# Eight attention heads as one four-phase pipeline, and TensorE's order written down, in a hybrid decoder layer

## The chip, the cores and the metric

The kernel runs on one core of a Trainium2 chip. The metric is the device time of one execution in microseconds (us). The engines are named as in the profile: PE is TensorE (matmuls), PEld its weight loads, DVE is VectorE, ACT is ScalarE, POOL is GpSimd, SP is SyncE, which issues most transfers.

## What is computed

One decoder layer on 256 tokens of width 1024, in float32. Two token mixers read the same input x through one wide projection: HGRN2, a gated linear recurrence with 8 heads, and MoBA, a causal attention with 8 heads of 128. Each is projected to the full width, weighted with a sigmoid gate per channel (gates a and b), summed and projected out; then come a LayerNorm, a SwiGLU feed-forward and a second LayerNorm. The 256 tokens are one block of MoBA (its block size is 256), so no past block can be selected, and its part comes down to plain causal attention:

```
q_b, k_b = rope(mq), rope(mk)
s = q_b @ k_b.T * 128**-0.5          # causal
y_b = softmax(s) @ mv                # per head
z_a, z_b = y_a @ w_branch_a, y_b @ w_branch_b
g_a, g_b = split(sigmoid(gate_logits + b_gate))
x = layer_norm(alpha * x + (g_a * z_a + g_b * z_b) @ w_out)
```

## The kernel before

A float32 value is held as the sum of a high and a low part, each in a format (float32r) that TensorE multiplies fast; a product of two such values takes three matmuls (high by high, high by low, low by high). Some small products are done in plain float32, and the profile shows each of those as two rows.

Weights stream in tiles of 128 x 2048 (1 MB). A tile is loaded by SP into one of three `raw` buffers, cast by ScalarE into one of four `wh` buffers (line 220), and VectorE subtracts to get the low part into one of four `wl` buffers (line 222). The function `stage` does that; `fetch` keeps it up to three tiles ahead of the tile in use. Tile number 29 is so the user of the same `wh` buffer as tile 33.

The products come in chunks. `tok_chunk` works on 512 output columns with two tiles: for each tile a half chunk of 24 matmuls of 512 columns, and after each half it yields, so that the caller can let other work in with `side.step()`. `wide_pair` makes one tile's 256 columns, transposed, with alternating matmuls of 512 and 256 columns; `rope_pair` uses it for two heads' keys or queries, with copies and adds on ScalarE and VectorE, the sine part of the rope on GpSimd (lines 695 and 696).

The order of the program's stages around the change: the first half of the values (`mv`, two tiles), gate b, keys and queries of heads 0 to 3 (`mk`, `mq`), the second half of the values, keys and queries of heads 4 to 7, gate a (`ga`, tiles 28 to 31), the projection of HGRN2's output (`za`, tiles 32 to 35), then that of MoBA's (`zb`). `side` holds generators from which each `step` takes one piece: first HGRN2's steps, then MoBA's heads.

A head (`moba_head`) is scores (`s`, lines 700 to 707, of split keys kh, kl and split queries qh, ql), softmax on VectorE and ScalarE in place (`ms`, with the statistics `st`), transposes of the probabilities (`pt`, line 723), their split (pTh, pTl, p1) and the product with the values (`po`, lines 731 to 734), whose split is ybh, ybl. Before, a head has two phases, and four heads at a time are interleaved two by two.

In this part of the program no engine's order is written down: a scheduler with its own estimate of times sets it for all engines, and may put any instruction between others as their data allow. Each engine then works its list strictly in order, and waits for others by semaphores. Sections under `tc.manual_schedule(engines=...)` keep the order of the code on the engines named; the stages from the last half of `zb` on are of that kind.

Of the kernel before, what the change touches and what calls it, by code (L numbers as in the profile page):

```python
# [11 lines left out]
F32R = mybir.dt.float32r  # L12
U32 = mybir.dt.uint32
AF = mybir.ActivationFunctionType
# [3 lines left out]
P = 128  # L18
T = 256
# [3 lines left out]
H = 8  # L23
# [15 lines left out]
HOLD_DOWN = 3  # L39
SUMS = 2  # L40
ORDERED = 2
DOWN = "SSPSTSTSPPP"
SUMS_AFTER = (8,12)
FAST = tuple(range(2, 2 + len(DOWN) - DOWN.count("P")))
# [81 lines left out]
def hybrid_layer_kernel(ctx: ExitStack, tc, x, xw, vecs, bias, wts, ln1_w, ln1_b, ln2_w, ln2_b, consts, out):  # L126
    nc = tc.nc
# [6 lines left out]
    sm = pool("sm", 2)  # L134
    klp = pool("klp", 1)
    mm = pool("mm", 4, space=PSUM)
# [54 lines left out]
    def split(dst_h, dst_l, src):  # L191
        nc.scalar.copy(dst_h, src)
        nc.vector.tensor_sub(dst_l, src, r32(dst_h))
# [94 lines left out]
    xp = Pair("xp")  # L288
# [35 lines left out]
    def wide_pair(name, a, p, tag, twos=0):  # L324


        wh, wl = fetch()
        pss = []
        for f in range(2):
            ps = p.tile([P, 2, T], F32, tag=tag, name=f"{name}{f}")  # L330
            wcol = slice(f * P, (f + 1) * P)
            n = twos if f == 0 else 0
            for ks in [(k, k + 1) for k in range(0, 2 * n, 2)] + [(k,) for k in range(2 * n, KC)]:
                for k in ks:
                    nc.tensor.matmul(ps, wh[:, k, wcol], a.both(k), start=(k == 0), stop=False)  # L335
                for k in ks:
                    nc.tensor.matmul(ps[:, 0, :], wl[:, k, wcol], a[0, k, slice(0, T)],  # L337
                                     start=False, stop=(k == KC - 1))
            pss.append(ps)
        return pss  # L340
# [36 lines left out]
    def tok_chunk(name, evac, ah=None, al=None):  # L377
        ah, al = (xTh, xTl) if ah is None else (ah, al)
        pss = [mm.tile([P, 512], F32, tag="mm", name=f"{name}_{t}") for t in range(NT)]
        for q in range(2):  # L380
            wh, wl = fetch()
            for t in range(NT):
                ts = slice(t * P, (t + 1) * P)
                for k in range(4):
                    kk = 4 * q + k
                    nc.tensor.matmul(pss[t], ah[:, kk, ts], wh[:, k, :], start=(kk == 0), stop=False)  # L386
                    nc.tensor.matmul(pss[t], al[:, kk, ts], wh[:, k, :], start=False, stop=False)  # L387
                    nc.tensor.matmul(pss[t], ah[:, kk, ts], wl[:, k, :], start=False, stop=(kk == KC - 1))  # L388
            if q == 1:
                for t in range(NT):  # L390
                    evac(t, pss[t])
            yield
# [16 lines left out]
    ET = mybir.EngineType  # L409
# [216 lines left out]
    side = Steps()  # L626
# [17 lines left out]
    def values(c):  # L644
        cs = slice(c * 512, (c + 1) * 512)

        def evac(t, ps):
            if t == 0:
                split(mvh[:, cs], mvl[:, cs], ps)
            else:  # L650
                nc.scalar.copy(mv1[:, cs], ps)

        for _ in tok_chunk(f"mv{c}", evac):
            side.step()

    values(0)

    def gates(name, b0):
        bgr = cp.tile([P, D], F32, tag="bgr", name=f"b{name}")
        tc.keep_in_program_order(nc.sync.dma_start(bgr, bias[:, b0:b0 + D]))  # L660
        g = slot(name).rearrange("p (t d) -> p t d", t=NT)
        for c in range(2):
            cs = slice(c * 512, (c + 1) * 512)

            def evac(t, ps):
                nc.vector.tensor_add(g[:, t, cs], ps, bgr[:, cs])
                nc.scalar.activation(g[:, t, cs], g[:, t, cs], AF.Sigmoid)

            for _ in tok_chunk(f"{name}{c}", evac):
                side.step()  # L670
        return g
# [9 lines left out]
    def rope_pair(nm, dst, j):  # L681
        if j == 0:
            ps = feat_pair(f"m{nm}{j}")
        else:
            ps = sm.tile([P, 2, T], F32, tag="sg", name=f"z{nm}{j}")
            for f, parts in enumerate(wide_pair(f"m{nm}{j}", xp, mm, "mm", {1: 1, 2: 2}.get(j, 0) if nm == "k" else 0)):
                nc.scalar.copy(ps[:, f, :], parts[:, 1, :])
                nc.vector.tensor_add(ps[:, f, :], parts[:, 0, :], ps[:, f, :])
        hs = slice(2 * j, 2 * j + 2)
        bc = lambda z: z[:, None, :].to_broadcast([P, 2, T])  # L690
        tmp = sm.tile([P, 2, T], F32, tag="sg", name=f"rt{nm}{j}")
        nc.scalar.copy(tmp[0:64], ps[64:P])
        nc.scalar.copy(tmp[64:P], ps[0:64])
        nc.vector.tensor_mul(dst[:, hs, :], ps, bc(cos))
        nc.gpsimd.tensor_mul(tmp, tmp, bc(sin))
        nc.gpsimd.tensor_add(dst[:, hs, :], dst[:, hs, :], tmp)

    def moba_head(h):
        ps = aux.tile([P, 3 * P], F32, tag="aux", name=f"s{h}")
        nc.tensor.matmul(ps[:, 0:P], qT[:, h, 0:P], kT[:, h, 0:P], start=True, stop=True)  # L700
        (kh, kl), (qh, ql) = [[sm.tile([P, n], F32R, tag=f"{tag}{z}", name=f"{nm}{z}{h}") for z in "hl"]
                              for nm, n, tag in (("k", T, "pT"), ("q", P, "q"))]
        split(kh, kl, kT[:, h, :])
        split(qh, ql, qT[:, h, P:T])
        nc.tensor.matmul(ps[:, P:3 * P], qh, kh, start=True, stop=False)
        nc.tensor.matmul(ps[:, P:3 * P], qh, kl, start=False, stop=False)
        nc.tensor.matmul(ps[:, P:3 * P], ql, kh, start=False, stop=True)
        s = sm.tile([P, 3 * P], F32, tag="ms", name=f"ms{h}")
        st = sm.tile([P, 8], F32, tag="st", name=f"st{h}")
        nc.vector.tensor_tensor(s, ps, causal, op=ALU.add)  # L710
        nc.vector.reduce_max(st[:, 0:1], s[:, 0:P], axis=mybir.AxisListType.X)
        nc.vector.reduce_max(st[:, 1:2], s[:, P:3 * P], axis=mybir.AxisListType.X)
        nc.vector.tensor_scalar(st[:, 2:4], st[:, 0:2], -SCALE, None, op0=ALU.mult)
        p = s
        nc.scalar.activation(p[:, 0:P], s[:, 0:P], AF.Exp, bias=st[:, 2:3], scale=SCALE, accum_out=st[:, 4:5])
        nc.scalar.activation(p[:, P:3 * P], s[:, P:3 * P], AF.Exp, bias=st[:, 3:4], scale=SCALE, accum_out=st[:, 5:6])
        nc.vector.reciprocal(st[:, 6:8], st[:, 4:6])
        nc.vector.tensor_scalar(p[:, 0:P], p[:, 0:P], st[:, 6:7], None, op0=ALU.mult)
        nc.vector.tensor_scalar(p[:, P:3 * P], p[:, P:3 * P], st[:, 7:8], None, op0=ALU.mult)
        yield  # L720
        pt = aux.tile([P, 3 * P], F32, tag="aux", name=f"pt{h}")
        for b in range(3):
            nc.tensor.transpose(pt[:, b * P:(b + 1) * P], p[:, b * P:(b + 1) * P], ident)
        pTh = sm.tile([P, T], F32R, tag="pTh", name=f"pTh{h}")
        pTl = sm.tile([P, T], F32R, tag="pTl", name=f"pTl{h}")
        p1 = sm.tile([P, P], F32, tag="pT", name=f"p1{h}")
        split(pTh, pTl, pt[:, 0:T])
        nc.scalar.copy(p1, pt[:, T:3 * P])
        hd = slice(h * P, (h + 1) * P)
        po = aux.tile([P, T], F32, tag="aux", name=f"po{h}")  # L730
        nc.tensor.matmul(po, mvh[:, hd], pTh, start=True, stop=False)
        nc.tensor.matmul(po, mvl[:, hd], pTh, start=False, stop=False)
        nc.tensor.matmul(po[:, P:T], mv1[:, hd], p1, start=False, stop=False)
        nc.tensor.matmul(po, mvh[:, hd], pTl, start=False, stop=True)
        split(ybh[:, h, :], ybl[:, h, :], po)
        yield

    def moba_heads(h0, n):
        heads = [moba_head(h) for h in range(h0, h0 + n)]
        next(heads[0])  # L740
        for i in range(n):
            if i < n - 1:
                next(heads[i + 1])
            next(heads[i])
            yield

    for c in range(2):
        if c == 1:
            values(1)
        for j in range(2 * c, 2 * c + 2):  # L750
            rope_pair("k", kT, j)
            side.step()
            rope_pair("q", qT, j)
            side.step()
        side.gens.append(moba_heads(4 * c, 4))
    ga = gates("ga", 0)


    side.step()
    for c in range(2):  # L760
        cs = slice(c * 512, (c + 1) * 512)
        for _ in tok_chunk(f"za{c}", lambda t, ps: nc.vector.tensor_mul(ga[:, t, cs], ps, ga[:, t, cs]), yah, yal):
            side.step()
    side.drain()
    mTh = slot("mTh", F32R).rearrange("p (k t) -> p k t", k=KC)
    mTl = slot("mTl", F32R).rearrange("p (k t) -> p k t", k=KC)

# [381 lines left out]
```

## Time and profile before

| | us |
|---|---|
| median of 3 runs | 493.35 |
| lowest, highest | 492.74, 493.41 |
| the profiled execution | 493.46 |
| its span, first to last instruction | 491.7 |
| TensorE busy in it | 484.4 |
| VectorE, ScalarE busy | 406.5, 297.5 |

The profile's page lists what each engine was busy with; its tables give groups of equal instructions with their count, their mean length and the idle time of the engine just ahead of them, with the work that ended it after an arrow. A table of stretches gives the engines' busy time in windows of the span. The list in order of time gives the start and the length of each instruction. Matmuls are pipelined and overlap in that list: what one costs is the distance from its start to the next one's.

### The profile page before, as it was taken

What the parts mean: (1) busy time and instruction counts of PE and PEld (TensorE: products, weight loads), DVE (VectorE), ACT (ScalarE), POOL (GpSimd) and SP (SyncE); (2) the same over time, 40 slices, a digit from 0 to 9 for tenths busy, and PEclk for the clock granted to TensorE, in tenths of its full rate; (3) what the DMA queues carried; (4) which work ended last, traced back from release to release, by engine and by line L of the source; (5) the groups of instructions that cost most, each with busy time, mean ns of one, the idle gap of its engine ahead of it and who ended that gap; (6) DMA issues with size and microseconds to landing.
All of it is one profiled execution on the core that took longest, in us unless ns stands there. A gap on an engine that the chain in (4) does not pass through costs nothing.

```text
span 491.7 us, 6779 instructions
## 1 busy us (share of the span) xinstructions
PE 484.4 (99%) x2621; PEld 418.2 (85%) x2621; DVE 406.5 (83%) x523; ACT 297.5 (61%) x415; POOL 41.6 (8%) x46
## 2 busy tenths in 40 slices
PE   9999999999999999999999999999999999999994
PEld 9889888888899888888888888888888888888784
DVE  5879899999667998988765678856897878989996
ACT  6698587435756767777653462544655655576663
POOL 0000000000004441240000000000000000000030
PEclk9999999999999999999999999999999999999999
DMA  8977426644552346349544455247859644267852
GB/s 314 420 285 261 172 93 249 227 159 171 172 171 87 136 167 239 122 162 337 179 165 171 167 181 232 101 176 276 318 219 338 214 171 173 91 231 244 317 145 85
DMA packets 17631, 99.99 MB, mean 203 GB/s; under 512 B 1984, under 2 KB 3776, under 8 KB 7616
## 3 DMA queue, kind: packets, MB, share of 16 engines
q1 hardware_dynamic: 14400, 92.62, 51.9%
q0 software_dynamic: 3056, 6.82, 4.2%
q8 instruction: 20, 0.33, 0.3%
q10 hardware_dynamic: 144, 0.13, 0.1%
q14 instruction: 11, 0.09, 0.0%
HBM read 94.84 MB, written 3.15 MB: 199 GB/s over the span
## 4 chain that ended last, share of the span: by engine, by line
PE 90%; DVE 5%; issue 2%; ACT 1%; DMA 1%; DVEq 0%; POOLq 0%; POOL 0%; ACTq 0%
PE fu L335 7%; PE fg L335 7%; PE fg L337 3%; PE fu L337 3%; PE mk L335 2%; PE mq L335 2%; PE hq L335 2%; PE sc L542 2%; PE ga L387 1%; PE hf L360 1%; PE ga L388 1%; PE ga L386 1%; PE za L386 1%; PE za L387 1%; PE mv L386 1%
## 5 line engine op out<-in xcount | busy, mean ns | idle before, releaser
L222 DVE TENSOR_TENSOR wl<-raw,wh 128x2048 fp32r<-128x2048 f32 (+1 forms) x71 | 162.4, 2293 | 48.2 <-ACT wh L220 47.9
L220 ACT CAST wh<-raw 128x2048 fp32r<-128x2048 f32 (+1 forms) x71 | 133.7, 1890 | 62.2 <-PE fg L335 14.2
L335 PE MATMUL fg<-x1p,wh 128*128 128x512 f32 x144 | 50.5, 394 | 0.0
L335 PE MATMUL fu<-x1p,wh 128*128 128x512 f32 x144 | 50.4, 394 | 0.0
L337 PE MATMUL fg<-x1p,wl 128*128 128x256 f32 x144 | 40.0, 278 | 0.0
L337 PE MATMUL fu<-x1p,wl 128*128 128x256 f32 x144 | 39.9, 277 | 0.0
L335 PEld LDWEIGHTS fu<-x1p,wh 128*128 128x128 f32 x144 | 27.0, 187 | 6.2
L335 PEld LDWEIGHTS fg<-x1p,wh 128*128 128x128 f32 x144 | 27.0, 187 | 6.1
L337 PEld LDWEIGHTS fg<-x1p,wl 128*128 128x128 f32 x144 | 27.1, 188 | 0.1
L337 PEld LDWEIGHTS fu<-x1p,wl 128*128 128x128 f32 x144 | 27.1, 188 | 0.0
L335 PE MATMUL mq<-xp,wh 128*128 128x512 f32 x48 | 17.2, 396 | 0.0
L335 PE MATMUL mk<-xp,wh 128*128 128x512 f32 x48 | 17.0, 397 | 0.0
L589 POOL TENSOR_TENSOR ost<-ost,half 128x4 f32<-128x4 f32 x4 | 4.1, 1015 | 152.7 <-DVE ost L588 152.7
L335 PE MATMUL hq<-xp,wh 128*128 128x512 f32 x48 | 16.7, 394 | 0.0
L337 PE MATMUL mq<-xp,wl 128*128 128x256 f32 x48 | 13.5, 282 | 0.0
L337 PE MATMUL hq<-xp,wl 128*128 128x256 f32 x48 | 13.3, 277 | 0.0
L337 PE MATMUL mk<-xp,wl 128*128 128x256 f32 x48 | 13.1, 284 | 0.0
L388 PE MATMUL ga<-wl,xp 128*128 128x512 f32 x32 | 12.7, 398 | 0.0
L387 PE MATMUL za<-wh,yal 128*128 128x512 f32 x32 | 12.7, 397 | 0.0
L879 PE MATMUL fe<-wh,x1p 128*128 128x512 f32 x32 | 12.6, 395 | 0.0
L388 PE MATMUL gb<-wl,xp 128*128 128x512 f32 x32 | 12.6, 395 | 0.0
L805 PE MATMUL wo<-wh,mTh 128*128 128x512 f32 x32 | 12.6, 394 | 0.0
(379 smaller groups left out, 1367.9 us busy)
## 6 DMA issues: line engine op xcount, KB each, us to landing
raw<-in_wts_dram SPq DMA_DIRECT2D x69, 1024.0 KB, 4.8
rawcorners<-in_wts_dram SPq DMA_DIRECT2D x5, 1024.0 KB, 4.8
xw<-in_xw_dram SPq DMA_DIRECT2D x6, 640.0 KB, 8.8
rawahead<-in_wts_dram SPq DMA_DIRECT2D x2, 1024.0 KB, 4.9
rawsums<-spill SPq DMA_DIRECT2D x2, 1024.0 KB, 4.8
rawcorners<-in_wts_dram SPq DMA_DIRECT2D x2, 768.0 KB, 5.9
raw<-in_wts_dram SPq DMA_DIRECT2D x2, 512.0 KB, 11.8
xr<-in_x_dram POOLq DMA_DIRECT2D x1, 1024.0 KB, 5.4
```

The source lines that it names most:

```text
L220: nc.scalar.copy(h[:, ks, :], raw[:, ks, :])
L222: eng.tensor_sub(l[:, ks, :], raw[:, ks, :], r32(h[:, ks, :]))
L335: nc.tensor.matmul(ps, wh[:, k, wcol], a.both(k), start=(k == 0), stop=False)
L337: nc.tensor.matmul(ps[:, 0, :], wl[:, k, wcol], a[0, k, slice(0, T)], start=False, stop=(k == KC - 1))
L360: nc.tensor.matmul(ps, wh[:, kk, wcol], xp.both(k), start=False, stop=False)
L386: nc.tensor.matmul(pss[t], ah[:, kk, ts], wh[:, k, :], start=(kk == 0), stop=False)
L387: nc.tensor.matmul(pss[t], al[:, kk, ts], wh[:, k, :], start=False, stop=False)
L388: nc.tensor.matmul(pss[t], ah[:, kk, ts], wl[:, k, :], start=False, stop=(kk == KC - 1))
L542: nc.tensor.matmul(ps[:, a, :], KL[:, h, :], later(Qt, n, h, 1), start=True, stop=True)
L589: nc.gpsimd.tensor_tensor(st[:, 8:12], st[:, 4:8], half, op=ALU.pow)
L805: nc.tensor.matmul(ps, lh(kk)[:, ts], wh[:, k, ns], start=(kk == first), stop=False)
L879: nc.tensor.matmul(ps, x1p[0, kk, ts], wh[:, k, :], start=(kk == 0), stop=False)
```

## The change

It does five things. `moba_head` gets two more places where it yields, so that a head has four phases: splits of key and query; scores and softmax; transposes and split of the probabilities; output product. `moba_heads` takes all eight heads, and a step takes, for each lag in `LAGS`, one phase of a different head: the output of head i − 5, the transposes of head i − 3, the scores of head i − 1, the splits of head i. The split keys move into one tile of four parts. The stages from the second half of the values to the end of `za` stand under a manual schedule for TensorE alone, so that TensorE keeps the order of the code, and the steps of the heads stand as blocks between half chunks and rope pairs; the other engines' order is still the scheduler's. Gate a's sigmoid is one operation on 2048 columns instead of four on 512, placed behind all exponentials. And in the wide products the first two matmuls of 512 columns go ahead of their two of 256 in other places than before.

```
+LAGS = (0,1,3,5)
...
-    def gates(name, b0):
+    def gates(name, b0, late=False):
...
                 nc.vector.tensor_add(g[:, t, cs], ps, bgr[:, cs])
-                nc.scalar.activation(g[:, t, cs], g[:, t, cs], AF.Sigmoid)
+                if not late:
+                    nc.scalar.activation(g[:, t, cs], g[:, t, cs], AF.Sigmoid)
...
-            for f, parts in enumerate(wide_pair(f"m{nm}{j}", xp, mm, "mm", {1: 1, 2: 2}.get(j, 0) if nm == "k" else 0)):
+            for f, parts in enumerate(wide_pair(f"m{nm}{j}", xp, mm, "mm", int(nm == "k" or j > 1))):
...
-    def moba_head(h):
+    def moba_head(h, keys):
+        kh, kl = [keys[:, 2 * (h % 2) + z, :] for z in range(2)]
+        qh, ql = [sm.tile([P, P], F32R, tag=f"q{z}", name=f"q{z}{h}") for z in "hl"]
+        split(kh, kl, kT[:, h, :])
+        split(qh, ql, qT[:, h, P:T])
+        yield
         ps = aux.tile([P, 3 * P], F32, tag="aux", name=f"s{h}")
         nc.tensor.matmul(ps[:, 0:P], qT[:, h, 0:P], kT[:, h, 0:P], start=True, stop=True)
-        (kh, kl), (qh, ql) = [[sm.tile([P, n], F32R, tag=f"{tag}{z}", name=f"{nm}{z}{h}") for z in "hl"]
-                              for nm, n, tag in (("k", T, "pT"), ("q", P, "q"))]
-        split(kh, kl, kT[:, h, :])
-        split(qh, ql, qT[:, h, P:T])
...
         nc.scalar.copy(p1, pt[:, T:3 * P])
+        yield
         hd = slice(h * P, (h + 1) * P)
...
-    def moba_heads(h0, n):
-        heads = [moba_head(h) for h in range(h0, h0 + n)]
-        next(heads[0])
-        for i in range(n):
-            if i < n - 1:
-                next(heads[i + 1])
-            next(heads[i])
+    def moba_heads(lags):
+        keys = klp.tile([P, 4, T], F32R, tag="kl", name="keys")
+        heads, n = [moba_head(h, keys) for h in range(H)], H
+        for i in range(n + lags[-1]):
+            for lag in lags[::-1]:
+                if 0 <= i - lag < n:
+                    next(heads[i - lag])
             yield
...
+    keys_queries(0)
+    side.gens.append(moba_heads(LAGS))
+    with tc.manual_schedule(engines={ET.PE}):
+        values(1)
+        keys_queries(1)
+        ga = gates("ga", 0, late=True)
+
+
+        side.step()
+        nc.scalar.activation(ga, ga, AF.Sigmoid)
+        for c in range(2):
+            cs = slice(c * 512, (c + 1) * 512)
+            for _ in tok_chunk(f"za{c}", lambda t, ps: nc.vector.tensor_mul(ga[:, t, cs], ps, ga[:, t, cs]), yah, yal):
+                side.step()
+        side.drain()
```

(`keys_queries(c)` is the loop over rope pairs that stood in the old code, with its steps.) Line numbers of the changed kernel are higher by 1 at the weight tiles (220 is 221) and by 7 at the scores (700 is 707).

What this does to the lists of the engines is shown at two places around gate a's second half chunk. The first is ScalarE's list before, from a weight cast to the next. The names are the tiles, with the number of the head or weight tile in them (qh6: head 6's query, high part; wh33: weight tile 33).

```order
L192 CAST kh5_2058<-kT_1319 128x256
L192 CAST qh6_2135<-qT_1318 128x128
L220 CAST wh33_2175<-raw33_2174 128x2048
L192 CAST ybh_1320<-po3_1888 128x256
L667 ACTIVATE ga_1999<-ga_1999 128x512
L192 CAST qh7_2208<-qT_1318 128x128
```

And ScalarE's list after the change, at the same weight tile:

```order
L193 CAST keys_1598<-kT_1319 128x256
L731 COPY p13_2037<-pt3_2031 128x128
L221 CAST wh33_2137<-raw33_2136 128x2048
L193 CAST qh6_2057<-qT_1318 128x128
L193 CAST qh7_2128<-qT_1318 128x128
L718 ACTIVATE ms5_2046,st5_2047<-ms5_2046,st5_2047 128x128
```

Head 6's query cast has moved from ahead of the cast of tile 33 to behind it. On VectorE the low part of the same query moves likewise; its list after the change:

```order
L667 TENSOR_TENSOR ga_1991<-ga0_1_1993,bga_1989 128x512
L223 TENSOR_TENSOR wl33_2138<-raw33_2136,wh33_2137 128x2048
L194 TENSOR_TENSOR ql6_2058<-qT_1318,qh6_2057 128x128
L194 TENSOR_TENSOR ql7_2129<-qT_1318,qh7_2128 128x128
```

Before, ql6 stood four rows ahead of wl33. The second place is TensorE's list, from the end of gate a's second half chunk, before:

```order
L387 MATMUL ga0_1_2001<-wh29_1897,xp1_87 128x512
L388 MATMUL ga0_1_2001<-wl29_1898,xp1_87 128x512
L386 MATMUL ga1_0_2172<-wh30_1948,xp0_86 128x512
L387 MATMUL ga1_0_2172<-wh30_1948,xp0_86 128x512
L733 MATMUL po3_1888<-p13_1884,mv1_959 128x128
L734 MATMUL po3_1888<-pTl3_1883,mv_958 128x256
L700 MATMUL s5_2056<-kT_1319,qT_1318 128x128
L388 MATMUL ga1_0_2172<-wl30_1949,xp0_86 128x512
L386 MATMUL ga1_0_2172<-wh30_1948,xp0_86 128x512
```

and after:

```order
L388 MATMUL ga0_1_1993<-wh29_1818,xp1_87 128x512
L389 MATMUL ga0_1_1993<-wl29_1819,xp1_87 128x512
L735 MATMUL po2_2095<-pTh2_1961,mv_958 128x256
L736 MATMUL po2_2095<-pTh2_1961,mv_958 128x256
L737 MATMUL po2_2095<-p12_1963,mv1_959 128x128
L738 MATMUL po2_2095<-pTl2_1962,mv_958 128x256
L726 MATMUL pt4_2102<-cst_89,ms4_1972 128x128 x3
L707 MATMUL s6_2112<-kT_1319,qT_1318 128x128
L708 MATMUL s6_2112<-keys_1598,qh6_2057 128x256
L709 MATMUL s6_2112<-keys_1598,qh6_2057 128x256
L710 MATMUL s6_2112<-keys_1598,ql6_2058 128x256
```

Before, pieces of heads (here head 3's output and head 5's first scores) are strewn among gate a's matmuls, and head 6's scores come only in the projection `za`; now head 2's output product, head 4's transposes and head 6's scores stand as one block right behind the half chunk that reads tile 29 last.

More of the change, by code (lines that the diff above doesn't have):

```diff
@@ L736, in moba_head, with keys_queries @@
         yield
-    def moba_heads(h0, n):
-        heads = [moba_head(h) for h in range(h0, h0 + n)]
-        next(heads[0])
-        for i in range(n):
-            if i < n - 1:
-                next(heads[i + 1])
-            next(heads[i])
+    def moba_heads(lags):
[5 more added lines that the diff above has]
+                    next(heads[i - lag])
             yield
-    for c in range(2):
-        if c == 1:
-            values(1)
+    def keys_queries(c):
         for j in range(2 * c, 2 * c + 2):
@@ L754, in hybrid_layer_kernel @@
             side.step()
[L755 to L764, printed above, removed]
+    keys_queries(0)
[11 more added lines that the diff above has]
+        side.drain()
     mTh = slot("mTh", F32R).rearrange("p (k t) -> p k t", k=KC)
```

## The prediction

> **What bounds the kernel now.** I read the page first, then the table of stretches, the waits of TensorE, and at the end the rows of the MoBA stage in order of time. The first fence is from the page: the span, the engines' busy time, the slices, the shares of the chain that ended last.
>
> ```profile
> span 491.7 us, 6779 instructions
> ...
> PE 484.4 (99%) x2621; PEld 418.2 (85%) x2621; DVE 406.5 (83%) x523; ACT 297.5 (61%) x415; POOL 41.6 (8%) x46
> ...
> PE 90%; DVE 5%; issue 2%; ACT 1%; DMA 1%; DVEq 0%; POOLq 0%; POOL 0%; ACTq 0%
> ```
>
> The second is the table of stretches (columns: the stretch, its length, busy time of each engine, granted clock, DMA), two of whose rows lie in the MoBA stage, with the only wait of TensorE that the trace lists.
>
> ```profile
> core 0: us, PE busy (x) PEld busy (x) DVE busy (x) ACT busy (x) POOL busy (x), PEclk, DMA share, GB/s
> 200.00:220.00 20.00, 20.00 (x109) 17.09 (x108) 17.98 (x28) 15.31 (x27) 8.81 (x7) 1.00 0.43 158
> 220.00:240.00 20.00, 20.00 (x101) 16.82 (x100) 16.00 (x32) 14.51 (x27) 1.10 (x2) 1.00 0.78 270
> ```
>
> ```profile
> PE warm L429 <- PEq L1136: 0.8, 1, 0.8
> ```
>
> TensorE never stops in this stage: 20.00 of 20.00 us, twice, at the full clock, and its one wait of 0.8 us is at the start. So the kernel is the sum of TensorE's matmuls. The change leaves every matmul in place. What it can win is the little that interleaving costs; what it can lose is any wait, one for one, because nothing behind is slack for TensorE to catch up in.
>
> **The change part by part.** First, the order on TensorE. Today the scheduler places a head's small matmuls where their operands have long been ready. Now a step of the pipeline stands as one block behind each half chunk (24 matmuls of 512 columns) or each rope pair, and TensorE waits there for whatever isn't ready. So I looked in the new order for operands that other engines make late, and found one that cannot be early: head 6's query split. On ScalarE the cast qh6 stood just ahead of the weight cast wh33; now it stands just behind. On VectorE ql6 stood four rows ahead of wl33; now it stands just behind. And the cast wh33 cannot start before TensorE has read wh29 for the last time, since the two share one of four buffers. That last read is the last but one matmul of gate a's second half chunk, and head 6's scores stand right behind that half chunk in TensorE's new order, with only head 2's output products and head 4's transposes between.
>
> The prices: first groups of the stage (line, engine, operation, out and in, shapes, count, busy us, mean ns, idle before), then rows in order of time (start, length).
>
> ```profile
> L220 ACT CAST wh<-raw 128x2048 fp32r<-128x2048 f32 x17 | 32.5, 1913 | 7.7 <-PE mv L387 2.9 <-PE mk L335 1.5 <-PE mq L347 1.2
> L715 ACT ACT_TABLE_LOAD x3 | 3.8, 1283 | 0.1
> L667 ACT ACT_TABLE_LOAD x2 | 2.6, 1283 | 0.0
> L667 ACT ACTIVATE ga<-ga 128x512 f32<-128x512 f32 x4 | 2.5, 636 | 0.8 <-DVE ga L666 0.8
> ```
>
> ```profile
> L713 DVE TENSOR_SCALAR st<-st 128x2 f32<-128x2 f32 x8 | 3.4, 434 | 0.0
> ```
>
> ```profile
> 220.06 0.39 ACT L192 CAST kh<-kT 128x256 fp32r<-128x256 f32 x1
> 220.35 0.30 ACT L192 CAST qh<-qT 128x128 fp32r<-128x128 f32 x1
> 220.82 1.92 ACT L220 CAST wh<-raw 128x2048 fp32r<-128x2048 f32 x1 [0.17 <-PE ga L387]
> ...
> 227.83 1.89 ACT L220 CAST wh<-raw 128x2048 fp32r<-128x2048 f32 x1
> ```
>
> ```profile
> 226.24 0.28 DVE L193 TENSOR_TENSOR ql<-qT,qh 128x128 fp32r<-128x128 f32 x1
> ...
> 229.75 2.29 DVE L222 TENSOR_TENSOR wl<-raw,wh 128x2048 fp32r<-128x2048 f32 x1 [1.05 <-ACT wh L220]
> 231.96 0.16 DVE L717 RECIPROCAL st<-st 128x2 f32<-128x2 f32 x1
> ```
>
> ```profile
> 176.38 0.39 PE L700 MATMUL s<-kT,qT 128*128 128x128 f32 x2
> 176.53 0.36 PE L705 MATMUL s<-kh,qh 128*128 128x256 f32 x1
> 176.73 0.28 PE L706 MATMUL s<-kl,qh 128*128 128x256 f32 x1
> 176.84 0.28 PE L707 MATMUL s<-kh,ql 128*128 128x256 f32 x1
> ...
> 220.40 0.39 PE L387 MATMUL ga<-wh,xp 128*128 128x512 f32 x1
> 220.62 0.39 PE L388 MATMUL ga<-wl,xp 128*128 128x512 f32 x1
> 220.85 0.40 PE L386 MATMUL ga<-wh,xp 128*128 128x512 f32 x1
> ...
> 221.31 0.38 PE L733 MATMUL po<-p,mv 128*128 128x128 f32 x2
> 221.45 0.36 PE L734 MATMUL po<-pTl,mv 128*128 128x256 f32 x1
> 221.65 0.38 PE L700 MATMUL s<-kT,qT 128*128 128x128 f32 x2
> ...
> 237.69 0.28 PE L731 MATMUL po<-pTh,mv 128*128 128x256 f32 x1
> 237.81 0.28 PE L732 MATMUL po<-pTh,mv 128*128 128x256 f32 x1
> 237.93 0.39 PE L700 MATMUL s<-kT,qT 128*128 128x128 f32 x2
> ```
>
> ```profile
> 186.63 0.33 PE pt L723 x3
> ```
>
> Matmuls overlap, so TensorE's pace is the distance of starts. Call M the start of the last matmul that reads wh29. In the trace of before that is the row at 220.40: it ends at 220.79, and the cast of tile 33 starts at 220.82. TensorE's own road from M: to the end of the half chunk 220.85 − 220.40 = 0.45; head 2's four output products 0.24 (237.69 to 237.93) and 0.34 (221.31 to 221.65); three transposes, 0.33 in the chain's row behind these; the scores up to their last matmul, the only one that reads ql6, 0.46 (176.38 to 176.84). It is there at M + 1.82, and at the first one that reads qh6 some 0.23 before (two spacings of 0.12, 176.73 to 176.84), at M + 1.59.
>
> The operands' road: wh33 runs from M + 0.42 to M + 2.34 (220.82 + 1.92); qh6 overlaps its end by 0.10 (220.06 + 0.39 against 220.35) and takes 0.30, so M + 2.54, and 0.03 later TensorE may go on: it has waited 0.98. VectorE starts wl33 at M + 2.37 (227.83 + 1.89 = 229.72, next start 229.75), 2.29, then ql6 with an overlap of 0.08 (232.04 against 231.96) and 0.28: M + 4.86, with the step M + 4.89. In all TensorE waits 4.89 − 1.82 = 3.07 us. Only the weight split's own two operations and head 6's two set this number, so I take it with small bounds: 2.8 if the small matmuls are slower than taken, 3.4 if ScalarE or VectorE is still at something else when its turn comes. Behind the waiting matmul stands all of TensorE; VectorE and ScalarE wait for it in turn, and SP's next weight load waits for wl33 as it does today.
>
> Second, fewer breaks. From the second half of the values on, the heads' work now enters as 18 runs of full-precision matmuls in place of 27 (counted in the two orders). In the rows above L700's pair to L707 is 0.46, which is 2 × 0.11 and 2 × 0.12: a break shows no more than 0.02. The dearest reading is L705 behind L700, 0.36 against 0.28 for L706, 0.08 a break. So nine breaks fewer give 0.1 to 0.7; I take 0.1, since spacings count and not lengths.
>
> Third, other thin places. VectorE is busy 17.98 of 20.00 where the last rope pairs run, and a 128x2 operation of the softmax takes 434 ns in the mean, though it is as small as the reciprocal of 0.16. Head 4's ql4, which now stands behind the weight split wl30 and five small operations, and head 7's softmax, with one half chunk between its scores and its transposes, may each be some tenths late. Nothing in the trace shows these waits. The eight slow operations took 3.4 us where 8 × 0.16 is 1.3, so 2.1 of such delay lies in the whole stage, at most half of it ahead of these two places: between 0 and 1.1 I take 0.2.
>
> Fourth, ScalarE. Ten table loads become seven, 3 × 1.28 = 3.85 us, and four sigmoids of 0.64 become one of the size of a weight cast, about 1.9 against 2.5. ScalarE isn't what TensorE waits for, so I cost this at nothing; the load and the sigmoid, 3.2 together, stand ahead of the casts for head 6's output, which TensorE reads a half chunk (24 × 0.23 = 5.5) later, and gate a is multiplied only after 48 matmuls of za. If that cover went, head 6's output would be late next.
>
> Fifth, GpSimd and SP. The load of xr now stands between the two halves of the last query's rope, which feeds qh6:
>
> ```profile
> 217.36 1.29 POOL L696 TENSOR_TENSOR qT<-qT,rtq 128x512 f32<-128x512 f32 x1
> 218.60 0.92 POOL L836 DMA_DIRECT2D xr<-in_x_dram  x1
> ```
>
> The issue takes 0.92, so the query is ready near 219.6 where it was 218.65, still ahead of a cast that ends near M + 2.3, 222.7. Cost nothing; cover 3 us. SP's list is the same row for row. The pairing in the wide products (two of 512 columns, then two of 256) moves no work: nothing. The keys' splits now share one tile in four parts, two a head, so a head's split waits for the scores of the head two before; ScalarE and VectorE wait there, with a step to spare: nothing.
>
> Sum: 3.07 + 0.2 − 0.1 = +3.2 us. The profiled execution took 493.46 (span 491.7 and 1.8 around it), so 496.65; it is 0.11 above the median of 493.35, for which I say 496.5. With the bounds above the case spans +2.1 (2.8 − 0.7) to +4.4 (3.4 + 1.1 − 0.1): 495.4 to 497.8.
>
> **The rivals.** A, no wait at head 6: this is decided by one thing, whether wh33 starts 3.1 us before M's end. If it did, say because its buffer were free a half chunk earlier, qh6 and ql6 would be there in time, and 0.1 to 0.7 from the breaks less 0.2 would stay: about 493.2, no change. For it speaks that TensorE waits nowhere today; against it the row at 220.82, whose idle time ended with gate a's own matmul.
>
> B, ScalarE is the bound: then three loads fewer win 3.85, 489.5. The rows speak against it: 14.51 of 20.00 busy and TensorE without a gap. The Trainium skill, "ScalarE: Activation LUTs", section "What ACT_TABLE_LOAD costs", gives 2.66 us for a switch, drain included, and by it the win would be 8.0 us, 485.4. The trace shows 1.28 us for a load.
>
> C, the clock falls in the wait. TensorE would stand 0.98, do two matmuls, and stand 2.1 more.
>
> ```profile
> 484.00:486.00 2.00, 1.27 (x11) 1.06 (x9) 1.88 (x5) 1.88 (x7) 0.00 (x0) 1.00 0.35 131
> 486.00:488.00 2.00, 0.00 (x0) 0.00 (x0) 1.62 (x6) 0.05 (x1) 0.55 (x1) 1.00 0.34 131
> 488.00:490.00 2.00, 0.00 (x0) 0.00 (x0) 0.54 (x1) 0.00 (x0) 0.00 (x0) 0.97 0.63 237
> ```
>
> Idle from about 485.3, TensorE keeps the full clock past 488, so 3.1 us of near idleness should not lower it. If it did for about the same time, 3.4 us at half speed, that is 1.7 more: 498.2. The Trainium skill, "TensorE: Matmul & The Clock Gate", section "HAM oscillation — how this bites in real kernels", warns of gaps over some 3.4 us; by that rule this gap is just too short, and the rows agree as far as they go.
>
> **How the numbers follow.** My forecast 0.84, A 0.08, B 0.01, C 0.07. A measurement of this kernel can tell about 0.2%, 1.0 us, from no change. Slower is the forecast, C: 0.91. A is mostly no change: 0.06 of it, with 0.02 faster; with B faster is 0.03. The range 494.8 to 498.3 holds the forecast's own, widened by half a microsecond downwards for what I haven't seen, and most of C.
>
> **What would show it.** In the profile after, the list of TensorE's waits should have two new rows in head 6's scores, one for ScalarE's qh near 1.0 us and one for VectorE's ql near 2.1, and near 220 us a slice with TensorE idle for 3 us; ScalarE should show seven table loads and less busy time, with nothing gained by it; the stretches before 200 us should be as they were. I am wrong if TensorE shows no gap there, if the gap is elsewhere, or if the clock of that slice is under 1.00.

## The result and the profile after

The changed kernel takes 498.80 us in the median (498.59 to 499.78) against 493.36 for the kernel before: 1.0118 times as long, 95% interval 1.0106 to 1.0130, or 5.4 us more. The forecast was 496.5, at most 498.3: the right sign and the right place, but only three fifths of the loss. The profiled execution, 498.93 with a span of 497.2, is compared with the span of 491.7 before. First its page, then TensorE's waits, then the two stretches of the MoBA stage (columns as in the prediction).

```profile
span 497.2 us, 6767 instructions
...
PE 486.0 (98%) x2621; PEld 419.5 (84%) x2621; DVE 405.4 (82%) x523; ACT 292.5 (59%) x409; POOL 42.5 (9%) x46
...
PE 81%; DVE 9%; ACT 4%; issue 2%; DMA 2%; POOL 1%; DVEq 0%; POOLq 0%; ACTq 0%
```

```profile
PE s L710 <- DVE ql L194: 2.1, 1, 2.1
PE pt L726 <- DVE ms L721: 1.7, 1, 1.7
PE warm L430 <- PEq L1144: 0.8, 1, 0.8
PE hf L358 <- ACT fh L193: 0.3, 1, 0.3
```

```profile
200.00:220.00 20.00, 19.96 (x112) 17.21 (x111) 18.53 (x37) 15.45 (x33) 8.64 (x5) 1.00 0.45 156
220.00:240.00 20.00, 16.15 (x76) 13.27 (x76) 14.07 (x30) 8.00 (x20) 3.37 (x5) 0.91 0.62 218
```

The loss lies in the second stretch. (The wait of 0.3 us at `hf` is in the first 20 us of the run, far ahead of what the change touches; TensorE's idle time in the whole span grew by 3.9 us, about the waits of this stretch alone.) TensorE is busy 16.15 of 20.00 us there, so 3.85 us are waits; and its granted clock, 1.00 before, is 0.91. The clock shows in the sum as well: TensorE is busy 486.0 us in all where it was 484.4, with the same 2621 matmuls. 3.85 + 1.6 is the 5.5 by which the span grew. ScalarE's seven table loads and 5 us less busy time bought nothing.

The list in order of time shows the two waits (in brackets behind a row) and, a microsecond after the second, matmuls of 512 columns with starts 0.43 us apart in place of 0.23:

```profile
220.05 0.39 PE L388 MATMUL ga<-wh,xp 128*128 128x512 f32 x1
...
220.88 0.36 PE L738 MATMUL po<-pTl,mv 128*128 128x256 f32 x1
222.99 0.61 PE L726 MATMUL pt<-cst,ms 128*128 128x128 f32 x3 [1.75 <-DVE ms L721]
...
223.78 0.28 PE L709 MATMUL s<-keys,qh 128*128 128x256 f32 x1
226.16 0.38 PE L710 MATMUL s<-keys,ql 128*128 128x256 f32 x1 [2.10 <-DVE ql L194]
...
227.08 0.54 PE L387 MATMUL ga<-wh,xp 128*128 128x512 f32 x1
227.42 0.63 PE L388 MATMUL ga<-wh,xp 128*128 128x512 f32 x1
227.85 0.63 PE L389 MATMUL ga<-wl,xp 128*128 128x512 f32 x1
...
230.41 0.47 PE L389 MATMUL ga<-wl,xp 128*128 128x512 f32 x1
230.72 0.40 PE L387 MATMUL ga<-wh,xp 128*128 128x512 f32 x1
```

The first row here is the last matmul that reads wh29, the M of the prediction. The wait for ql6 has the length that was forecast, 2.10 where 2.09 was worked out, but it comes about in another way, as told further below. The wait of 0.98 for qh6 is not there; a longer one, 1.75, stands before it, at head 4's transposes. Its cause is in the same view on VectorE and GpSimd, with ScalarE's weight cast and query casts for the second wait:

```profile
220.72 1.85 DVE L194 TENSOR_TENSOR keys<-kT,keys 128x256 fp32r<-128x256 f32 x1
222.50 0.15 DVE L716 TENSOR_SCALAR st<-st 128x2 f32<-128x2 f32 x1
222.57 0.27 DVE L721 TENSOR_SCALAR ms<-ms,st 128x128 f32<-128x128 f32 x1
...
223.03 0.67 DVE L667 TENSOR_TENSOR ga<-ga,bga 128x512 f32<-128x512 f32 x1
223.63 2.27 DVE L223 TENSOR_TENSOR wl<-raw,wh 128x2048 fp32r<-128x2048 f32 x1
225.83 0.48 DVE L194 TENSOR_TENSOR ql<-qT,qh 128x128 fp32r<-128x128 f32 x2
...
218.06 2.06 POOL L697 TENSOR_TENSOR rtq<-rtq,cst 128x512 f32<-128x512 f32 x1 [3.84 <-ACT rtq L695]
220.06 0.92 POOL L844 DMA_DIRECT2D xr<-in_x_dram  x1
221.01 1.28 POOL L698 TENSOR_TENSOR qT<-qT,rtq 128x512 f32<-128x512 f32 x1
...
221.00 1.90 ACT L221 CAST wh<-raw 128x2048 fp32r<-128x2048 f32 x1
222.80 0.50 ACT L193 CAST qh<-qT 128x128 fp32r<-128x128 f32 x2
```

The low part of a key, 0.42 us in its median row, took 1.85 here and ended 0.28 after GpSimd's add on the queries. Head 4's scaling (L721), for which TensorE waited, stands two rows behind it. And GpSimd's add came so late because its product ended only at 220.12 and the issue of xr, 0.92 us, stood between the two. One thing these rows leave open: the key's row begins 0.29 before the add's, and it was held all the same.

### The profile page after: what moved, and what is told of

Read it like the earlier page. It is cut to its first block, busy times and chain, and to the rows that moved or that the text cites. A ratio compares the mean times of both kernels' runs of the same rounds, so it can differ in the third digit from the quotient of the medians.

```text
span 497.2 us, 6767 instructions
## 1 busy us (share of the span) xinstructions
PE 486.0 (98%) x2621; PEld 419.5 (84%) x2621; DVE 405.4 (82%) x523; ACT 292.5 (59%) x409; POOL 42.5 (9%) x46
## 4 chain that ended last, share of the span: by engine, by line
PE 81%; DVE 9%; ACT 4%; issue 2%; DMA 2%; POOL 1%; DVEq 0%; POOLq 0%; ACTq 0%
PE fu L336 7%; PE fg L336 7%; PE fg L338 3%; PE fu L338 3%; DVE wl L223 3%; PE hq L336 2%; PE sc L543 2%; ACT wh L221 2%; PE hf L361 1%; PE fe L889 1%; PE mv L387 1%; PE gb L387 1%; PE za L387 1%; PE gb L388 1%; PE fe L887 1%
## 5 line engine op out<-in xcount | busy, mean ns | idle before, releaser
L388 PE MATMUL ga<-wh,xp 128*128 128x512 f32 x32 | 13.2, 413 | 0.0
L387 PE MATMUL ga<-wh,xp 128*128 128x512 f32 x32 | 13.1, 410 | 0.0
```

## Experiments

From here on two theories are told apart. Theory W with its parts: the loss is two waits and a fall of the clock behind them; what stands ahead of head 6's query makes the waits, and VectorE is held while GpSimd works (called theory H below). Its rival: blocks of small matmuls in a written order cost by themselves. Each kernel was timed beside the kernel before, whose median was 493.12 in the first four experiments and 493.38 in the other four.

| kernel | median, us | ratio to before, 95% interval | waits of TensorE in the stage, us |
|---|---|---|---|
| changed kernel | 498.80 | 1.0118 (1.0106 to 1.0130) | 1.75 and 2.10 |
| xr_behind | 494.50 | 1.0030 (1.0019 to 1.0040) | 0.94 |
| fill_waits | 497.54 | 1.0089 (1.0075 to 1.0103) | filled |
| one_step_later | 494.50 | 1.0026 (1.0016 to 1.0036) | 1.28 |
| order_free | 492.96 | 0.9996 (0.9987 to 1.0005) | none |
| fill_first | 499.54 | 1.0126 (1.0111 to 1.0141) | 2.11 |
| fill_second | 497.46 | 1.0081 (1.0068 to 1.0094) | 1.75 |
| hold_twice | 496.55 | 1.0064 (1.0048 to 1.0080) | 2.01 |
| later_scaled | 493.86 | 1.0007 (0.9999 to 1.0016) | 0.37 |

**xr_behind: one row of GpSimd moved.**

```
-    nc.gpsimd.dma_start(xr, x.rearrange("(t p) d -> p t d", p=P))
+    tc.keep_in_program_order(nc.gpsimd.dma_start(xr, x.rearrange("(t p) d -> p t d", p=P)))
```

> The changed kernel with one row moved: GpSimd issues the load of xr behind the last query's rope add instead of ahead of it. On ScalarE the casts qh6 and qh7 then stand ahead of the cast of tile 33, on VectorE ql6 and ql7 ahead of wl33; TensorE's list is the same row for row. Theory W (the 5.4 us are two waits of TensorE, 1.75 + 2.10, and the clock that falls behind them, 1.65; all of it comes from what stands ahead of head 6's query): the wait of 2.10 is gone, the add ends near 221.4 instead of 222.29, so the 1.85 us operation on the keys ends some 0.9 earlier and the wait for head 4's softmax shrinks from 1.75 to 0.9; with one short wait the clock stays at 1.00. 498.8 - 2.1 - 0.85 - 1.65 = 494.2, between 493.3 and 495. Rival S (the loss is in the blocks on TensorE themselves): the waits come back at other heads, 497 or more. Rival X (the issue costs only its own 0.92): 497.9.

494.50: 4.3 us of the 5.4 are gone with this one row. The first fence is all that its list of TensorE's waits has in the stage; the clock stays at 1.00. The second, its rows in order of time, shows GpSimd's add starting at 220.24, the key's low part taking 1.03 instead of 1.85 on VectorE, and ql6 behind it with only three small operations between, instead of behind the weight split:

```profile
PE pt L726 <- DVE ms L721: 0.9, 1, 0.9
```

```profile
220.24 1.28 POOL L698 TENSOR_TENSOR qT<-qT,rtq 128x512 f32<-128x512 f32 x1
221.47 0.92 POOL L844 DMA_DIRECT2D xr<-in_x_dram  x1
...
220.77 1.03 DVE L194 TENSOR_TENSOR keys<-kT,keys 128x256 fp32r<-128x256 f32 x1
...
222.40 0.48 DVE L194 TENSOR_TENSOR ql<-qT,qh 128x128 fp32r<-128x128 f32 x2
```

So the wait of 2.10 came from the order of the query's split and the weight's, and that order from xr, since both lists turned round with this one row. Why is not shown, as the scheduler's estimates are not in the record; most likely it took the query for late and so placed the weight split ahead of it. Head 4's wait shrank by 0.81, from 1.75 to 0.94, about the issue's 0.92. Theory W holds to 0.3 us; Rivals S (497 or more) and X (497.9) do not.

**fill_waits, fill_first, fill_second: idle work in the waits.** The first kernel has both of these edits, the other two one each.

```
+        for _ in range(18 if h == 6 else 0):
+            nc.tensor.transpose(ps[:, 0:P], ident, ident)
         nc.tensor.matmul(ps[:, 0:P], qT[:, h, 0:P], kT[:, h, 0:P], start=True, stop=True)
...
+        for _ in range(15 if h == 4 else 0):
+            nc.tensor.transpose(pt[:, 0:P], ident, ident)
         for b in range(3):
```

> The changed kernel with idle work on TensorE just where it waits: 15 transposes of the identity (0.11 us apart, 1.65 in all) ahead of head 4's transposes, into the same tile, and 18 (1.98) ahead of head 6's scores; nothing reads them. The other engines' lists are the same row for row. Theory K (the clock falls because TensorE stood still twice, 1.75 and 2.10 with 0.8 of work between): TensorE is busy throughout, the granted clock stays 1.00 from 227 to 231, and the time is 498.8 - 1.65 = 497.15, give or take 0.4. Rival K2 (the clock falls there for another reason): 498.8 and a clock near 0.5 from 227 to 231 as before. If the transposes cost more than the waits that they fill, up to 0.5 comes on top.

> The changed kernel with only the first wait filled: the 15 transposes of the identity ahead of head 4's transposes. The other engines' lists are the same. TensorE is left with one wait, the 2.1 us for ql6. Theory K3 (it takes both waits close together to lower the clock): clock 1.00 from 227 to 231, 498.8 - 1.65 = 497.15, or what fill_waits took, 497.5. Rival K4 (one wait of 2.1 is enough): 498.8, with a slice near 0.5.

> The changed kernel with only the second wait filled: the 18 transposes ahead of head 6's scores. TensorE is left with one wait, 1.75 us for head 4's softmax. Theory K3: clock 1.00 throughout, 497.2 to 497.5. Rival K4 with 1.75 enough: 498.8.

In the profile of the kernel with both waits filled, the operands come as late as before (the matmul that reads ql6 starts at 226.04; it was 226.16), but the clock stays up, and the ratio falls from 1.0118 to 1.0089, some 1.4 us. Two of its stretches, behind the place of the waits:

```profile
226.00:228.00 2.00, 1.96 (x9) 1.65 (x10) 1.97 (x8) 0.27 (x1) 0.00 (x0) 1.00 0.57 160
228.00:230.00 2.00, 2.00 (x11) 1.65 (x10) 0.82 (x4) 0.99 (x4) 0.00 (x0) 1.00 0.93 393
```

So the gaps lower the clock, and rival K2 is out. With only the first filled, the one wait of 2.11 is enough, against theory K3, and the time exceeds the 498.8 of K4; with only the second filled, the one of 1.75 is not. Of fill_first and then fill_second, the stretches behind the wait:

```profile
227.00:229.00 2.00, 2.00 (x7) 1.56 (x8) 1.97 (x8) 0.27 (x1) 0.00 (x0) 0.59 0.58 215
229.00:231.00 2.00, 2.00 (x7) 1.57 (x6) 0.82 (x5) 0.99 (x4) 0.00 (x0) 0.55 0.75 311
```

```profile
227.00:229.00 2.00, 2.00 (x10) 1.62 (x9) 1.97 (x7) 0.27 (x1) 0.00 (x0) 1.00 0.91 293
229.00:231.00 2.00, 2.00 (x11) 1.65 (x10) 0.81 (x5) 0.99 (x4) 0.00 (x0) 1.00 0.76 320
```

The two kernels differ by 2.1 us, of which the clock explains some 1.7 (3.4 us at half speed). The mean granted clocks of the single runs agree but for one: 0.997 to 0.999 in all runs of fill_waits and fill_second, 0.990 to 0.995 in those of the changed kernel, 0.992 or 0.993 in three of fill_first, and 0.997 in its fourth, which took 500.29. That fill_first's median is 0.7 above the changed kernel is not the fill's doing: in its profile the block already starts 0.66 later (head 2's first output product at 221.16; 220.50 in the changed kernel), and from there to the matmul that reads ql6 it takes 5.67, where the changed kernel takes 5.66. A wait at `hf`, 0.3 longer, is part of that delay; the rest is not explained, and the two intervals of the ratio overlap.

**hold_twice: does GpSimd hold VectorE?**

```
         nc.gpsimd.tensor_add(dst[:, hs, :], dst[:, hs, :], tmp)
+        if nm == "q" and j == 3:
+            nc.gpsimd.tensor_mul(tmp, tmp, bc(sin))
```

> The kernel xr_behind with one more product on GpSimd, as large as the rope's own (128x512, 1.29 us), right behind the last query's add; nothing reads it. ScalarE's, VectorE's and TensorE's lists are the same row for row. Theory H (a VectorE operation that works on operands in SBUF alone is held while GpSimd multiplies or adds): the small operation behind the keys' split, or the split itself, is held for another 1.3, TensorE's wait of 0.94 becomes 2.2, and the time 494.5 + 1.3 = 495.8, between 495.3 and 496.3. Rival H2 (the 1.85 and 1.03 us operations are late for another reason): no change, 494.5.

The wait grew from 0.94 to 2.01. The product that nobody reads runs as the second row here, and the small operation behind the key's split, 0.15 long when nothing is in its way, takes 1.23:

```profile
220.11 1.28 POOL L698 TENSOR_TENSOR qT<-qT,rtq 128x512 f32<-128x512 f32 x1
221.47 1.33 POOL L700 TENSOR_TENSOR rtq<-rtq,cst 128x512 f32<-128x512 f32 x1
...
220.64 1.03 DVE L194 TENSOR_TENSOR keys<-kT,keys 128x256 fp32r<-128x256 f32 x1
221.60 1.23 DVE L718 TENSOR_SCALAR st<-st 128x2 f32<-128x2 f32 x1
...
223.16 0.61 PE L728 MATMUL pt<-cst,ms 128*128 128x128 f32 x3 [2.01 <-DVE ms L723]
```

H2 is out: VectorE is held by GpSimd. But theory H as it was put, for every VectorE operation on SBUF alone, is too wide. In the profile of the changed kernel this row runs while GpSimd's product of 218.06 to 220.12 does, and takes no longer than its kind takes elsewhere (0.41 at 228.19):

```profile
219.08 0.41 DVE L715 TENSOR_REDUCE st<-ms 128x1 f32<-128x256 f32 x1
```

What was held in these runs are operations with two inputs from SBUF and those of the form TENSOR_SCALAR. The median, 496.55, lies above the expected range for a reason of its own: six runs took 495.27, 495.74 and 496.06, and 497.04, 497.55 and 497.95. The profile is of the run of 497.04 and shows a clock of 0.57 from 224 to 228. Three runs are where the wait alone puts them, three some 1.8 us above, so a wait of 2.0 seems to lower the clock in some executions and not in others. The mean granted clocks point the same way, 0.997 to 0.999 in the three short runs and 0.994 to 0.996 in the three long ones, but the kernel before shows 0.995 to 0.999 without such a step in its times, and of the other five runs there is no profile.

**one_step_later and later_scaled: the same work with more room.**

```
-LAGS = (0,1,3,5)
+LAGS = (0,2,4,6)
...
         ga = gates("ga", 0, late=True)
-        side.step()
```

> The changed kernel with LAGS = (0,2,4,6) in place of (0,1,3,5) and without the step between gate a and za: scores, transposes and output of every head come one or more half chunks (5.5 us) later behind its splits. The load of xr is left as it is. Theory W: head 6's scores come 5.5 us later, its query parts were 2.1 late, head 4's softmax gets as much more room; no wait of TensorE, no fall of the clock, 493.35 with 0.1 to 0.7 less for fewer breaks and 0.2 more for thin places: 492.7 to 493.7. Rival S (the blocks themselves cost): 496 or more.

Head 6 waits for nothing any more, but 494.50 misses the expected 492.7 to 493.7: a wait of 1.28 has come up at head 2's transposes. It is the same hold at another place, two rows of VectorE beside two of GpSimd, ahead of the scaling at 213.26:

```profile
209.33 2.17 POOL L697 TENSOR_TENSOR rtk<-rtk,cst 128x512 f32<-128x512 f32 x1 [3.57 <-ACT rtk L695]
211.57 1.28 POOL L698 TENSOR_TENSOR kT<-kT,rtk 128x512 f32<-128x512 f32 x1
...
210.25 1.27 DVE L716 TENSOR_SCALAR st<-st 128x2 f32<-128x2 f32 x1
...
211.83 1.17 DVE L194 TENSOR_TENSOR ql<-qT,qh 128x128 fp32r<-128x128 f32 x1
...
213.26 0.27 DVE L721 TENSOR_SCALAR ms<-ms,st 128x128 f32<-128x128 f32 x1
```

So later_scaled takes the scaling from VectorE, and moves xr as xr_behind does:

```
-        nc.vector.tensor_scalar(p[:, 0:P], p[:, 0:P], st[:, 6:7], None, op0=ALU.mult)
+        nc.scalar.activation(p[:, 0:P], p[:, 0:P], AF.Copy, scale=st[:, 6:7])
```

(and the second scaling likewise).

> The kernel one_step_later with the load of xr behind the rope's add, and the softmax's two scalings of each head on ScalarE (activation Copy with the scale) in place of VectorE: 16 operations move. Theory H (what is left in one_step_later, 1.28 us, is VectorE held by GpSimd ahead of head 2's scaling): the scaling no longer stands behind VectorE's held operations, TensorE waits for nothing, and only the breaks and the rest remain: 493.1 - 0.1 = 493.0, between 492.4 and 493.8. Rival (ScalarE becomes late in its place): a wait behind ScalarE, 494 to 495.5.

493.86, 0.06 above the range; the ratio cannot be told from 1. One wait of 0.37 is left, not behind ScalarE but behind VectorE's rope, and that stands behind a key's low part of 1.37 (at 204.85), beside GpSimd's add of 204.65 to 205.94. A written order of TensorE with hardly a wait is thus as fast as the kernel before, and no faster.

**order_free: the change without the written order.**

```
-    with tc.manual_schedule(engines={ET.PE}):
+    if True:
```

> The changed kernel without the written order on TensorE: the four phases, the keys in one tile and the single sigmoid stay, but the scheduler places TensorE's rows as in the kernel before. Theory W: the scheduler puts the small matmuls where their operands are ready by its estimate, TensorE waits for nothing over 0.5 us, 493.3 (492.8 to 494.3). Rival P (the phases cost, by the two halves of the key tile or by head 6's query behind the weight split, whoever orders TensorE): 495 to 499.

492.96, no difference from before. TensorE has no wait in the stage, and the four phases, the keys in one tile and the single sigmoid cost nothing. The kernel does not single out the written order, though: without it the scheduler also set xr's issue back behind the query's add (219.15 behind 217.91). On its page ScalarE is busy 3.8 us less than before, with nothing gained:

```profile
PE 484.1 (99%) x2621; PEld 418.2 (85%) x2621; DVE 406.9 (83%) x523; ACT 293.7 (60%) x410; POOL 39.7 (8%) x46
```

None of these kernels is measurably faster than the one before.

## Where the prediction held and where it failed

**What held.** The place: the block behind the second half chunk of gate a. Of the second wait, the order: ql6 behind wl33; xr_behind, where the query stands ahead of the weight split, has no such wait. ScalarE's saving at nothing: order_free. SP and the phases at nothing: order_free again. The breaks, 0.1 of gain: no run shows it; TensorE is busy 484.6 us in xr_behind and 484.2 in later_scaled, both with the fewer breaks, against 484.4 before.

**What held by luck.** That the second wait took 2.10 where 2.09 was worked out. The prediction had wl33 start as soon as wh33 ends, with nothing but the two splits and the two casts setting the number. But wh33 ended at 222.90 (221.00 + 1.90), and wl33 started only at 223.63, since VectorE was busy until then with head 4's scalings and gate a's add (L667), both behind the held key split. So ql6 came 1.22 us later after M than worked out (the matmul that reads it starts at M + 6.11, not at M + 4.89). TensorE, which had stood 1.75 for head 4, came there 1.21 later (M + 4.01, not M + 2.80). Both slips begin with the held key split; that they cancel to 0.01 us is chance. TensorE's last read of wh29, from which the prediction counted, was not what set the wait.

**First failed step: the fifth, "Cost nothing; cover 3 us".** It saw that xr's issue now stands ahead of the last query's add, worked out a query ready near 219.6, and asked only whether qh6 would be in time. The add ended at 222.29, and even so qh6 was in time: its cast started at 222.80, right behind wh33, and the wait of 0.98 stayed hidden behind head 4's. Two things were left out. GpSimd's product ahead of it (L697) had itself slipped, to 218.06 from 215.98 before, and took 2.06. And GpSimd's work holds VectorE, so the issue had a second customer: head 4's softmax. Moving that one row back is worth 4.3 us: 0.81 of head 4's wait, the 2.10 that the first step had priced without seeing that xr is behind it, and the clock. The fifth step priced xr at zero.

**Second: the third step, 0.2 for thin places.** It named ql4 and head 7, and head 4's transposes were the thin place. They cost 1.75, where the step had 0.2; since this wait hides the 0.98 for qh6, the waits came to 3.85, 0.8 more than the 3.07 of the sum. The clue stood in the prediction: eight operations of 128x2 with a mean of 434 ns where 160 would do. The text took this for a delay without a cause and spread it. Its cause was in the trace of before, had the rows in order of time been laid side by side (first fence: GpSimd's product stretched beside a weight split, then VectorE's small operations stretched beside the product), or two of its groups (second fence):

```profile
179.44 3.13 POOL L695 TENSOR_TENSOR rtq<-rtq,cst 128x512 f32<-128x512 f32 x1 [5.73 <-ACT rtq L693]
...
181.34 1.33 DVE L713 TENSOR_SCALAR st<-st 128x2 f32<-128x2 f32 x2
```

```profile
L193 DVE TENSOR_TENSOR kl<-kT,kh 128x256 fp32r<-128x256 f32 x8 | 4.9, 616 | 0.0
L193 DVE TENSOR_TENSOR pTl<-pt,pTh 128x256 fp32r<-128x256 f32 x8 | 3.3, 415 | 0.0
```

The same operation on the same size (the groups' last figures are busy time, mean and idle time) takes 616 ns in the mean when both inputs are in SBUF, and 415 when one is in PSUM. The median of the first group is 418 as well: six of the eight take 0.41 to 0.43, and two, at 163.11, take 2.35 together, beside GpSimd's work of 161.54 to 165.18. No row of the second group runs beside GpSimd's products or adds, so it is the long rows that are the clue, not the two means by themselves. The Trainium skill, "SBUF — State Buffer", section "Who interferes with whom", says that a VectorE instruction with two SBUF inputs contends with a GpSimd instruction that reads SBUF, that a tensor_scalar can contend with GpSimd in a mode that takes two ports, and that the one which issues second is blocked until the first has ended. hold_twice agrees: VectorE's operation, begun at 221.60, took 1.23 in place of 0.15 beside a GpSimd product of 1.33 that began at 221.47. The prediction should have drawn on it.

**Third: rival C was dismissed.** "Idle from about 485.3, TensorE keeps the full clock past 488, so 3.1 us of near idleness should not lower it." One gap at the end of the span, with a clock that happened to stay up, does not say how short a gap can lower it. In fill_first one wait of 2.11, begun at 224.7, lowered it at about 227.3; in fill_second one of 1.75 did not; in hold_twice 2.01 did, at least in the profiled run. The price was right: 1.7 forecast, 1.6 measured as TensorE's longer busy time. The Trainium skill, "TensorE: Matmul & The Clock Gate", section "HAM oscillation — how this bites in real kernels", sets the limit at gaps over some 3.4 us; the waits here are shorter, and the measurement decides. The Trainium skill, the same page, section "What's actually happening", tells of a window of 3.4 us that runs freely; half speed for about 3.4 us and a limit that moves between executions would fit that, but no run here sets the phase.

With these the sum comes out. Waits of 3.07 + 0.8 = 3.85 and 1.6 for the clock make 5.5, the growth of the span, where the prediction had 3.07 + 0.2 − 0.1 = 3.2. Of the 2.3 that were missing, the clock is the larger part. The clock's fall alone would have given the 498.2 of rival C; with head 4's wait on top it became 498.80.

## What to carry to other kernels

When one engine is busy without a gap and its order is about to be written down, price every operand that its blocks read, and look for who can hold each producer: here a DMA issue of 0.92 us on GpSimd delayed an add, the add held VectorE, and with the place of that issue two of the scheduler's lists turned round. A group of equal operations whose mean lies far above its median (here 616 and 418 ns) can be a sign of such a hold, and rows of the two engines laid side by side show it. And a long wait of TensorE can cost more than itself: here waits of 2.01 and 2.11 us cost some 1.7 us again through the clock, in part or all of the runs, and one of 1.75 did not. Whether several short waits close together do the same was not tried.

## What the runs showed of the hardware

- GpSimd's products and adds of 128x512 stop VectorE's operations with two inputs from SBUF and its TENSOR_SCALAR, and are stopped by them: VectorE's key split of 0.42 us became 1.85 and 1.03, its 0.15 became 1.23, GpSimd's product of 1.30 became 2.06 behind a weight split. A VectorE operation of 128x256 with an input in PSUM took its usual 0.40 at 219.47, and a TENSOR_REDUCE of 128x256 its usual 0.41 at 219.08, both beside GpSimd's product of 218.06 to 220.12.
- TensorE's clock fell to 0.5 for about 3.4 us after a wait of 2.11 (fill_first) and stayed up after waits of 0.94, 1.28 and 1.75. At 2.01 the six times lie in two groups, 495.3 to 496.1 and 497.0 to 498.0.
- Idle transposes in a wait keep the clock: the same waits filled cost 1.3 to 1.8 us less (medians, spans).
